# Scan's diagonal part: one masked exponential per direction, and the diagonal itself joined to the skip weight

## The chip, the cores and the metric

One core of a Trainium2 chip runs the whole layer. The metric is the device time of one execution in microseconds (us); lower is better. Before the change it is 2922.42 us, the median of three runs (2921.04 to 2922.88).

## What is computed

The kernel is one layer of a diffusion backbone over 2048 latent tokens (width 1024) and 256 context tokens. A projection feeds two branches: a gated MLP (gMLP) and a Mamba-2 scan (SSD) with 16 heads in two groups, run forwards and backwards over 16 chunks of 128 tokens. Both branches go through one output projection, and a SwiGLU feed-forward follows. What matters here is the scan inside a chunk:

```python
def _ssd_chunked(x, dt, A, bm, cm, h0):
    a = dt * A
    a_cs = jnp.cumsum(a, axis=2)
    xdt = x * dt[..., None]
    seg = a_cs[:, :, :, None] - a_cs[:, :, None, :]
    tri = jnp.tril(jnp.ones((SSD_CHUNK, SSD_CHUNK), dtype=bool))
    decay = jnp.exp(jnp.where(tri, seg, -jnp.inf))
    cb = jnp.einsum('bctgn,bcsgn->bctsg', cm, bm)
    y_diag = jnp.einsum('bctsg,bctsge,bcsgep->bctgep', cb, decay, xdt)
    ...
    y = y_diag + y_off

def _token_mixer(...):
    y, fin_f, fin_b = _ssd_bidirectional(xs, bm, cm, dt_raw, a_log, dt_bias, st_f, st_b)
    y = y.astype(h.dtype) + xs * d_skip[:, None]
```

So for each head the part of `y` inside a chunk is a 128 by 128 matrix times the chunk's `x`. Its entry for a pair of tokens s, t is `cb[t,s]` times the forward term `exp(a_cs[t]-a_cs[s])*dt_f[s]` where s is not after t, plus the mirrored backward term where s is not before t. On the diagonal (s = t) both exponentials are 1.

## The kernel before, in words

The order in which each engine gets its instructions is set when the program is built, by a scheduler that works through the code below; the code's generators (`run`, line 958) say how the main chain of projections and the scan's side chain alternate.

**Projections.** Every large matmul is done three times with split operands (`mm3`, line 224): high by high, high by low, low by high, 24 matmuls of 512 columns for one 128 by 512 output. Their results go to three PSUM banks (`mmp`); everything small uses five others (`smp`). TensorE runs these nearly without a break, and the rest of the kernel lies beside them.

**Conv and scan inputs** (`xbc`, line 474, run for tokens 1024 to 2047 first, then for 0 to 1023). For each 128-channel unit there are the projection, a five-tap convolution on VectorE (line 456), a SiLU, and `finish` (line 481). For the units of C, `finish` also multiplies B by C (lines 498 and 499, four matmuls into one `smp` bank), multiplies the result by a lower and an upper triangular mask on VectorE (line 502, masks with the diagonal) and writes both to a DRAM record `rec` (line 504). `dt_block` (line 401) makes the step sizes `dt_sb`, their running sums `acs`, the negative of the backward sums `nacs`, and the factors `eac`, `ddt`, `tot`; the sums also go to DRAM as rows (`fscr`).

**The scan's output** (`ssd_y`, line 852): 32 items, one for each chunk and group, worked on beside the projections `proj_v`, `proj_u` and `out_half` from about 790 to 1480 us. An item is loaded (`load_rec`, line 727: x, B, C and the two masked products, 1024 columns), then prepared by `y_seg` (line 767), and one item later finished by `y_out` (line 797). `y_seg` works in two quarters of four heads (two quarters an item, 64 in all). For each quarter `f_load` (line 757) fetches two tiles from `fscr`, the forward sums `fb` and the backward sums `bb`, broadcast over the partitions, 256 KB each. For each head of the quarter there are then four short instructions of 128 columns, two on ScalarE (lines 782 and 784) and two on VectorE (lines 783 and 785), and for the quarter one exponential of 512 columns on ScalarE (line 786) and one product on GpSimd (line 787):

```python
S.activation(bb[:, es], bb[:, es], AF.Identity, bias=nacs[:, c, h:h + 1])
V.scalar_tensor_tensor(out=fb[:, es], in0=fb[:, es], scalar=acs[:, c, h:h + 1], in1=bb[:, es], op0=ALU.subtract, op1=ALU.min)
S.activation(A[:, es], rc[:, R_WF:R_WF + P], AF.Copy, scale=dt_sb[:, c, h:h + 1])
V.scalar_tensor_tensor(out=A[:, es], in0=rc[:, R_WB:R_WB + P], scalar=dt_sb[:, c, 16 + h:17 + h], in1=A[:, es], op0=ALU.mult, op1=ALU.add)
```

`y_out` multiplies C by the states (lines 801 and 802), the quarter matrices by x (line 804), scales and adds the parts on VectorE (lines 807, 808, 815, 816, 818), carries the forward state on (lines 812 to 814; line 813 is on GpSimd), and adds the skip `xs*D` (line 817, GpSimd). `y_store` (line 828) transposes and stores. The tiles `tma` come from one ring of 14 that loads, scan and projections share.

## Time and profile before

| | |
|---|---|
| median of 3 runs | 2922.42 us (2921.04 to 2922.88) |
| the profiled execution | 2923.61 us, of which its span is 2921.8 us |
| TensorE (PE) busy | 2803.1 us, 96% of the span |
| VectorE (DVE) busy | 1975.6 us, 68% |
| ScalarE (ACT) busy | 1274.2 us, 44% |
| GpSimd (POOL) busy | 645.4 us, 22% |
| mean granted TensorE clock | 0.98 of full speed |

The page counts an engine as busy while an instruction of it runs; where two overlap in its pipeline the time counts once. "Idle before" is the time that an engine stood still just before an instruction, with what released it. PEclk is the TensorE clock that was granted in a stretch, as a share of 2.4 GHz; it stands at either 2.4 or 1.2 GHz, and 0.96 is a mean over time at the two. SP is the queue that issues most DMAs.

### The profile page before, as it was taken

Reading aid. Unit: us, or ns where it says so; the run is one execution under the profiler, and the core shown is the slowest. Engines: PE = TensorE matmul, PEld = TensorE weight load, DVE = VectorE, ACT = ScalarE, POOL = GpSimd, SP = SyncE. Lnnn points to the kernel's source line nnn. Section 1 sums busy time; section 2 is a strip of 40 time slices with the busy share of each in tenths; the row PEclk is TensorE's granted clock in tenths of the full one; section 3 lists DMA queues with packets and bytes.
Section 4 is the critical chain, followed back from the end, with each engine's and each line's share of the span. In section 5 each row is a group of like instructions: output and inputs, shape, how many; then the busy total and the mean of one; then the engine's idle time right before and its main releaser. Section 6 shows DMA issues by size and latency. Waiting matters only on the chain. (4 is left out here: it accounts for less than half of the span.)

```text
span 2921.8 us, 36695 instructions
## 1 busy us (share of the span) xinstructions
PE 2803.1 (96%) x12478; PEld 2242.7 (77%) x12478; DVE 1975.6 (68%) x3007; ACT 1274.2 (44%) x2361; POOL 645.4 (22%) x555
## 2 busy tenths in 40 slices
PE   7999999999999998998979899999999999999997
PEld 2788778888677776776768688888887788888886
DVE  6776866886678888678676765555876544445556
ACT  4445343344356555444443533333554333333443
POOL 3200000200032233232202444444211222221000
PEclk8999999999999999999989999999999999999998
DMA  6232567743664678787658444445775423334654
GB/s 228 89 94 78 193 226 243 252 127 91 224 187 145 185 253 269 230 268 235 211 178 282 170 156 149 165 154 181 256 249 195 133 102 101 108 109 136 224 192 162
DMA packets 296743, 528.02 MB, mean 181 GB/s; under 512 B 28998, under 2 KB 89830, under 8 KB 296556
## 3 DMA queue, kind: packets, MB, share of 16 engines
q1 hardware_dynamic: 255756, 505.48, 53.0%
q10 hardware_dynamic: 40800, 20.21, 2.4%
q8 instruction: 98, 1.61, 0.2%
q14 instruction: 89, 0.73, 0.1%
HBM read 382.94 MB, written 142.64 MB: 180 GB/s over the span
## 5 line engine op out<-in xcount | busy, mean ns | idle before, releaser
L1065 DVE TENSOR_TENSOR hl<-w,hl 128x1024 fp32r<-128x1024 f32 x286 | 372.1, 1306 | 300.8 <-ACT hl L1064 129.5
L1064 ACT CAST hl<-w 128x1024 fp32r<-128x1024 f32 x286 | 298.8, 1048 | 423.1 <-PE smp L1311 150.0
L234 PE MATMUL mmp<-actt,whi 128*128 128x512 f32 x1120 | 455.7, 407 | 13.3 <-DVE tma L932 8.7
L236 PE MATMUL mmp<-actt,wlo 128*128 128x512 f32 x1120 | 442.1, 395 | 0.0
L235 PE MATMUL mmp<-actt,whi 128*128 128x512 f32 x1120 | 441.5, 394 | 0.2 <-DVE actt L898 0.2
L1179 PE MATMUL mmp<-hl,hl 128*128 128x512 f32 x704 | 276.5, 393 | 2.6 <-ACT t L1204 2.6
L1181 PE MATMUL mmp<-hl,hl 128*128 128x512 f32 x704 | 275.7, 392 | 1.0 <-DVE hl L1065 1.0
L1180 PE MATMUL mmp<-hl,hl 128*128 128x512 f32 x704 | 275.6, 392 | 0.0
L234 PEld LDWEIGHTS mmp<-actt,whi 128*128 128x128 f32 x1120 | 213.7, 191 | 62.0 <-DVE tma L932 9.7
L235 PEld LDWEIGHTS mmp<-actt,whi 128*128 128x128 f32 x1120 | 213.8, 191 | 47.0 <-issue 4.3
L236 PEld LDWEIGHTS mmp<-actt,wlo 128*128 128x128 f32 x1120 | 213.2, 190 | 46.0 <-issue 0.2
L234 PE MATMUL mmp<-whi,actt 128*128 128x512 f32 x512 | 208.9, 408 | 2.9 <-DVE tma L698 2.9
L1180 PE MATMUL smp<-hl,hl 128*128 128x512 f32 x528 | 208.5, 395 | 3.0 <-DVE hl L1065 3.0
L1181 PE MATMUL smp<-hl,hl 128*128 128x512 f32 x528 | 208.2, 394 | 2.5 <-DVE hl L1065 2.5
L1179 PE MATMUL smp<-hl,hl 128*128 128x512 f32 x528 | 209.8, 397 | 0.4 <-ACT hl L1064 0.4
L235 PE MATMUL mmp<-wlo,actt 128*128 128x512 f32 x512 | 206.4, 403 | 0.5 <-DVE wlo L221 0.5
L236 PE MATMUL mmp<-whi,actt 128*128 128x512 f32 x512 | 206.0, 402 | 0.0
L1071 DVE TENSOR_TENSOR t<-smp,t 128x512 f32<-128x512 f32 x88 | 60.5, 687 | 181.1 <-PE smp L1181 131.4
L787 POOL TENSOR_TENSOR tma<-tma 128x512 f32<-128x512 f32 x64 | 93.4, 1461 | 339.4 <-ACT tma L786 138.4
L456 DVE SCALAR_TENSOR_TENSOR tma<-xin,cw,tma 128x512 f32<-128x512 f32 x192 | 144.3, 751 | 25.5 <-ACT tma L454 19.3
L1179 PEld LDWEIGHTS mmp<-hl,hl 128*128 128x128 f32 x704 | 132.7, 189 | 32.5 <-ACT t L1204 3.0
L1071 POOL TENSOR_TENSOR w<-w 128x512 f32<-128x512 f32 x44 | 58.9, 1339 | 446.2 <-DVE hl L1065 290.8
(276 smaller groups left out, 5809.0 us busy)
## 6 DMA issues: line engine op xcount, KB each, us to landing
w<-in_wall_dram SPq DMA_DIRECT2D x110, 512.0 KB, 3.8
ws<-in_wall_dram SPq DMA_DIRECT2D x104, 512.0 KB, 5.0
ascr<-t SPq DMA_DIRECT2D x154, 256.0 KB, 3.9
w<-ascr SPq DMA_DIRECT2D x154, 256.0 KB, 3.3
tma<-fscr SPq DMA_DIRECT2D x128, 256.0 KB, 5.7
w<-wscr SPq DMA_DIRECT2D x88, 256.0 KB, 3.0
t<-x2scr SPq DMA_DIRECT2D x76, 256.0 KB, 4.1
w<-in_wall_dram SPq DMA_DIRECT2D x66, 256.0 KB, 3.1
```

Of the source, the lines that this page charges most:

```text
L234: PE.matmul(ps, lhsT=lh, rhs=rh, start=(i == 0), stop=False)
L235: PE.matmul(ps, lhsT=lh, rhs=rl, start=False, stop=False)
L236: PE.matmul(ps, lhsT=ll, rhs=rh, start=False, stop=(i == n - 1))
L456: V.scalar_tensor_tensor(out=acc[:, :n], in0=raw[:, j:j + n], scalar=cw[:, ch, j:j + 1], in1=acc[:, :n], op0=ALU.mult, op1=ALU.add)
L787: G.tensor_tensor(out=A, in0=A, in1=fb, op=ALU.mult)
L1064: S.copy(hi, x)
L1065: eng.tensor_tensor(out=lo, in0=x, in1=hi.bitcast(F32), op=ALU.subtract)
L1071: eng.tensor_tensor(out=o, in0=a, in1=b, op=ALU.add)
L1179: PE.matmul(ps, lhsT=hi[:, ms_], rhs=t[:, 0, :], start=first and k == 0, stop=False, skip_group_check=not first)
L1180: PE.matmul(ps, lhsT=hi[:, ms_], rhs=t[:, 1, :], start=False, stop=False, skip_group_check=not first)
L1181: PE.matmul(ps, lhsT=lo[:, ms_], rhs=t[:, 0, :], start=False, stop=k == 3, skip_group_check=not first)
```

## The change

It rewrites the quarter of `y_seg` and what feeds it.

- In `finish` the product of B and C is copied once, without masks (ScalarE), and written once to the record, which shrinks from 1024 to 896 columns. The diagonal of the product is made apart: GpSimd multiplies B by C element by element into `dg`, and four matmuls of one column each sum `dg` over its partitions, into the bank that held the product; ScalarE copies the four columns to `cbd`.
- In `dt_block`, `nacs` becomes `ln(dt) - acs` for both directions (one more logarithm), and `dskip = cbd*(dt_f+dt_b) + D` is made for all chunks of the block (three VectorE instructions).
- In `y_seg` each direction gets a tile of 0 and -1e30 added (`cut`, without the diagonal), the forward one on GpSimd, the backward one on VectorE; eight exponentials of 128 columns on ScalarE follow, with `nacs` as bias, then one sum and one product with the record's `cb`, both 512 columns on VectorE. The tile `A` is no longer taken.
- In `y_out` the skip uses `dskip` in place of `D`.

```diff
@@ -75,9 +77,8 @@
-R_WF = 768
-R_WB = 896
-R_N = 1024
+R_CB = 768
+R_N = 896
@@ dt_block
         V.tensor_copy(acs[:, cs, :], v3(pi))
-        V.tensor_scalar(out=nacs[:, cs, :], in0=acs[:, cs, 16:32], scalar1=-1.0, scalar2=None, op0=ALU.mult)
+        V.tensor_scalar(out=v3(e), in0=dt, scalar1=TINY, scalar2=None, op0=ALU.max)
+        S.activation(e[:, :w], e[:, :w], AF.Ln)
+        V.tensor_tensor(out=nacs[:, cs, :], in0=v3(e), in1=acs[:, cs, :], op=ALU.subtract)
+        c8 = slice(c0, c0 + 8)
+        V.tensor_tensor(out=dskip[:, c8, :], in0=dt_sb[:, c8, 0:16], in1=dt_sb[:, c8, 16:32], op=ALU.add)
+        d4 = dskip[:, c8, :].rearrange("p a (g h) -> p a g h", g=2)
+        V.tensor_tensor(out=d4, in0=d4, in1=bc(cbd[:, c8, :].rearrange("p a (g o) -> p a g o", o=1), 8), op=ALU.mult)
+        V.tensor_tensor(out=dskip[:, c8, :], in0=dskip[:, c8, :], in1=row[:, 64:80].rearrange("p (o h) -> p o h", o=1).broadcast_to([P, 8, 16]), op=ALU.add)
@@ xbc, finish
-                    for roff, m in ((R_WF, C_LE), (R_WB, C_GE)):
-                        t = tma()
-                        V.tensor_tensor(out=t[:, :TB].rearrange("p (c x) -> p c x", x=P), in0=ps.rearrange("p (c x) -> p c x", x=P),
-                                        in1=masks[:, m:m + P].rearrange("p (o x) -> p o x", o=1).broadcast_to([P, 4, P]), op=ALU.mult)
-                        DMA.dma_start(rec[q][g][:, :, roff:roff + P].rearrange("c p x -> p c x"),
-                                      t[:, :TB].rearrange("p (c x) -> p c x", x=P))
+                    t = tma()
+                    S.copy(t[:, :TB], ps)
+                    dg = tma()
+                    G.tensor_tensor(out=dg[:, :TB], in0=bt[j][:, :TB], in1=o[:, :TB], op=ALU.mult)
+                    for c in range(4):
+                        PE.matmul(ps[:, c:c + 1], lhsT=dg[:, c * P:(c + 1) * P], rhs=ones[:, 0:1], start=True, stop=True)
+                    S.copy(cbd[:, q * 4:q * 4 + 4, g], ps[:, 0:4])
+                    DMA.dma_start(rec[q][g][:, :, R_CB:R_CB + P].rearrange("c p x -> p c x"),
+                                  t[:, :TB].rearrange("p (c x) -> p c x", x=P))
@@ y_seg
-            A = tma()[:, :TB]
-            for e in range(4):
-                es = slice(e * P, (e + 1) * P)
-                h = h0 + e
-                S.activation(bb[:, es], bb[:, es], AF.Identity, bias=nacs[:, c, h:h + 1])
-                V.scalar_tensor_tensor(out=fb[:, es], in0=fb[:, es], scalar=acs[:, c, h:h + 1], in1=bb[:, es], op0=ALU.subtract, op1=ALU.min)
-                S.activation(A[:, es], rc[:, R_WF:R_WF + P], AF.Copy, scale=dt_sb[:, c, h:h + 1])
-                V.scalar_tensor_tensor(out=A[:, es], in0=rc[:, R_WB:R_WB + P], scalar=dt_sb[:, c, 16 + h:17 + h], in1=A[:, es], op0=ALU.mult, op1=ALU.add)
-            S.activation(fb, fb, AF.Exp)
-            G.tensor_tensor(out=A, in0=A, in1=fb, op=ALU.mult)
-            Gt.append(A)
+            for x, o, eng in ((fb, 0, G), (bb, 16, V)):
+                x3 = x.rearrange("p (e t) -> p e t", t=P)
+                eng.tensor_tensor(out=x3, in0=x3, in1=cuts[0][:, o // 16:o // 16 + 1, :].broadcast_to([P, 4, P]), op=ALU.add)
+                for e in range(4):
+                    es = slice(e * P, (e + 1) * P)
+                    S.activation(x[:, es], x[:, es], AF.Exp, bias=nacs[:, c, o + h0 + e:o + h0 + e + 1])
+            V.tensor_tensor(out=fb, in0=fb, in1=bb, op=ALU.add)
+            f3 = fb.rearrange("p (e t) -> p e t", t=P)
+            V.tensor_tensor(out=f3, in0=f3, in1=rc[:, R_CB:R_CB + P].rearrange("p (o t) -> p o t", o=1).broadcast_to([P, 4, P]), op=ALU.mult)
+            Gt.append(fb)
@@ y_out
-        G.tensor_tensor(out=h3(yb), in0=h3(rc[:, R_X:R_X + TB]), in1=hv(row[:, 64 + g * 8:64 + g * 8 + 8]), op=ALU.mult)
+        G.tensor_tensor(out=h3(yb), in0=h3(rc[:, R_X:R_X + TB]), in1=hv(dskip[:, c, g * 8:g * 8 + 8]), op=ALU.mult)
@@ before the scan's stage
+    cut = hp.tile([P, 2, P], F32, name="cut")
+    for i, m in enumerate((C_LT, C_GT)):
+        V.tensor_scalar(out=cut[:, i, :], in0=masks[:, m:m + P], scalar1=BIG, scalar2=-BIG, op0=ALU.mult, op1=ALU.add)
```

Two places show how the change moves instructions. In the lists L is the line in the kernel at hand (the change's lines are numbered anew), and names are output and input tiles.

TensorE in the first `xbc`, where the one-column matmuls of the first two products stand. Before, the place held projections (L234 to L236) and four transposes (L468):

```order
L235 MATMUL mmp<-actt,whi 128x512
L236 MATMUL mmp<-actt,wlo 128x512
L234 MATMUL mmp<-actt,whi 128x512
L235 MATMUL mmp<-actt,whi 128x512
L468 MATMUL smp<-ident,tma 128x128 x4
L236 MATMUL mmp<-actt,wlo 128x512
L234 MATMUL mmp<-actt,whi 128x512
```

With the change (projections are L235 to L237, the transposes L478, the one-column matmuls L515):

```order
L236 MATMUL mmp<-actt,whi 128x512
L237 MATMUL mmp<-actt,wlo 128x512
L235 MATMUL mmp<-actt,whi 128x512
L515 MATMUL smp<-ones,tma 128x1 x4
L478 MATMUL smp<-ident,tma 128x128 x2
L515 MATMUL smp<-ones,tma 128x1 x4
L478 MATMUL smp<-ident,tma 128x128 x2
L236 MATMUL mmp<-actt,whi 128x512
```

Eight one-column matmuls came in between; nothing went out. They stand 82 and 68 projection matmuls behind the B by C products whose bank they write.

VectorE late in the scan's stage, from the last steps of one item's `y_out` (L823) over an item's `y_seg` to the first step of the next `y_out` (L807). Before:

```order
L823 TENSOR_TENSOR tma<-tma 128x512
L785 SCALAR_TENSOR_TENSOR tma<-rec_sb,dt_sb,tma 128x128
L932 SCALAR_TENSOR_TENSOR tma<-mmp,m_sb,tma 128x512
L783 SCALAR_TENSOR_TENSOR tma<-tma,acs 128x128 x2
L785 SCALAR_TENSOR_TENSOR tma<-rec_sb,dt_sb,tma 128x128
...
L783 SCALAR_TENSOR_TENSOR tma<-tma,acs 128x128
L785 SCALAR_TENSOR_TENSOR tma<-rec_sb,dt_sb,tma 128x128
L932 SCALAR_TENSOR_TENSOR tma<-mmp,m_sb,tma 128x512
L807 TENSOR_TENSOR tma<-smp,eac 128x512
```

With the change (L837 and L821 are the old L823 and L807, L946 the old L932, L265 a sum of squares; L795 adds `cut` to the backward tile, L799 is the sum, L801 the product):

```order
L837 TENSOR_TENSOR tma<-tma 128x512
L795 TENSOR_TENSOR tma<-tma,cut 128x512
L946 SCALAR_TENSOR_TENSOR tma<-mmp,m_sb,tma 128x512
L795 TENSOR_TENSOR tma<-tma,cut 128x512
L799 TENSOR_TENSOR tma<-tma 128x512
L265 TENSOR_TENSOR tma<-tma 128x512
L801 TENSOR_TENSOR tma<-tma,rec_sb 128x512
L799 TENSOR_TENSOR tma<-tma 128x512
L946 SCALAR_TENSOR_TENSOR tma<-mmp,m_sb,tma 128x512
L801 TENSOR_TENSOR tma<-tma,rec_sb 128x512
L821 TENSOR_TENSOR tma<-smp,eac 128x512
```

Sixteen short instructions became six long ones; the first step of the next `y_out` still stands behind the last of them.

## Rows read from the trace of the kernel before

**Rows 1.** The page's first part: busy time, share of the span, instructions.
```profile
PE 2803.1 (96%) x12478; PEld 2242.7 (77%) x12478; DVE 1975.6 (68%) x3007; ACT 1274.2 (44%) x2361; POOL 645.4 (22%) x555
```
**Rows 2.** Busy us (PE, PEld, DVE, ACT, POOL) in first xbc and scan's stage; clock, DMA.
```profile
100.00:280.00 180.00, 179.93 (x962) 154.11 (x961) 130.39 (x191) 82.33 (x153) 8.92 (x57) 0.99 0.30 93
790.00:1480.00 690.00, 649.68 (x2957) 511.16 (x2956) 545.90 (x1094) 362.79 (x973) 202.19 (x155) 0.96 0.71 220
```
**Rows 3.** TensorE's waits, 700 to 1480 us: total us, times, longest.
```profile
PE smp L845 <- DVE tma L807: 5.2, 2, 4.3
PE smp L802 <- DVE tma L807: 5.2, 1, 5.2
PE smp L801 <- issue: 4.6, 1, 4.6
PE mmp L234 <- DVE tma L592: 4.6, 3, 3.2
...
PE smp L804 <- POOL tma L787: 1.1, 1, 1.1
```
**Rows 4.** TensorE in time, first xbc: start, us, line, shape, count.
```profile
120.46 0.40 PE L236 MATMUL mmp<-actt,wlo 128*128 128x512 f32 x1
120.69 1.05 PE L499 MATMUL smp<-tma 128*128 128x128 f32 x8
121.50 0.48 PE L234 MATMUL mmp<-actt,whi 128*128 128x512 f32 x1
121.81 0.40 PE L235 MATMUL mmp<-actt,whi 128*128 128x512 f32 x1
```
**Rows 5.** The same, in an item's `y_out` at 1363 us.
```profile
1363.13 1.89 PE L804 MATMUL smp<-rec_sb,tma 128*128 128x64 f32 x16
1364.86 1.08 PE L812 MATMUL smp<-tma,rec_sb 128*128 128x512 f32 x2
```
**Rows 6.** ScalarE in time, `dt_block` of the second xbc, with the idle time before.
```profile
735.95 1.28 ACT L448 ACT_TABLE_LOAD   x1
740.11 0.38 ACT L448 ACTIVATE ddt<-smp 128x256 f32<-128x256 f32 x1 [2.88 <-PE smp L435]
```
**Rows 7.** VectorE by line, 790 to 1480 us: count, busy us, mean ns, idle before.
```profile
L785 DVE SCALAR_TENSOR_TENSOR tma<-rec_sb,dt_sb,tma 128x128 f32<-128x128 f32 x256 | 101.0, 419 | 15.1 <-ACT tma L784 14.9
L783 DVE SCALAR_TENSOR_TENSOR tma<-tma,acs 128x128 f32<-128x128 f32 x256 | 101.0, 418 | 60.7 <-ACT tma L782 56.8 <-DMA tma<-fscr 3.8
...
L818 DVE TENSOR_TENSOR tma<-tma 128x512 f32<-128x512 f32 x16 | 11.0, 689 | 3.8 <-POOL tma L817 3.4
```
**Rows 8.** ScalarE by line, the same stretch.
```profile
L782 ACT ACTIVATE tma<-tma,nacs 128x128 f32<-128x128 f32 x256 | 88.9, 390 | 91.7 <-DMA tma<-fscr 85.8 <-DMA tma<-hscr 4.7 <-issue 0.9
...
L786 ACT ACTIVATE tma<-tma 128x512 f32<-128x512 f32 x64 | 40.1, 627 | 47.1 <-DVE tma L783 43.1 <-issue 2.8 <-POOL h L813 1.2
```
**Rows 9.** GpSimd by line, the same stretch.
```profile
L787 POOL TENSOR_TENSOR tma<-tma 128x512 f32<-128x512 f32 x64 | 93.4, 1461 | 339.4 <-ACT tma L786 138.4 <-DMA zscr<-tma 75.0 <-DVE tma L785 63.1
```
**Rows 10.** VectorE in time: a run of five long instructions (L903).
```profile
1113.01 3.10 DVE L903 SCALAR_TENSOR_TENSOR actt<-xin,actt 128x512 fp32r<-128x512 f32 x5
```
**Rows 11.** VectorE in time: a run of three short instructions (L785).
```profile
907.96 0.86 DVE L785 SCALAR_TENSOR_TENSOR tma<-rec_sb,dt_sb,tma 128x128 f32<-128x128 f32 x3
```
**Rows 12.** ScalarE in time: a run of four short instructions (L784).
```profile
1370.69 1.28 ACT L784 ACTIVATE tma<-rec_sb,dt_sb 128x128 f32<-128x128 f32 x4 [2.64 <-DVE xin L895]
```
**Rows 13.** ScalarE's waits, 790 to 1480 us: total us, times, longest.
```profile
ACT tma L782 <- DMA tma<-fscr: 85.8, 39, 5.9
```
**Rows 14.** VectorE in time at 1155 us, instructions of 8 and of 128 columns.
```profile
1155.74 1.01 DVE L245 TENSOR_TENSOR sml<-sml 128x8 f32<-128x8 f32 x1
1156.67 0.34 DVE L785 SCALAR_TENSOR_TENSOR tma<-rec_sb,dt_sb,tma 128x128 f32<-128x128 f32 x1
1156.93 0.16 DVE L246 SCALAR_TENSOR_TENSOR sml<-sml 128x8 f32<-128x8 f32 x1
```
**Rows 15.** GpSimd in time, the same stretch.
```profile
1155.56 1.17 POOL L793 TENSOR_TENSOR tma<-rec_sb,ddt 128x512 f32<-128x512 f32 x1 [6.11 <-DVE sml L247]
```

8 lines of the change are left out of this document (7 added, 1 removed).

## The prediction, made before the changed kernel was run

> **What bounds the kernel now.** I read the page first. TensorE is busy for 2803.1 of 2921.8 us, no other engine for more than 1975.6 [rows 1], so time can change only where TensorE gets other instructions or stands still. The view by stretch then shows the two places that the change touches [rows 2]. In the first xbc TensorE is busy for 179.93 of 180 us: VectorE's or ScalarE's work there is hidden, and whatever is added to TensorE counts in full. In the scan's stage, 790 to 1480 us, it is busy for 649.68 of 690 us, so 40.3 us are idle, and its clock stands at 0.96. At two levels of 2.4 and 1.2 GHz that means 2 x 0.04 x 690 = 55 us at half speed, which cost 27.6 us. Together some 68 us lie open. The list of waits says who ends them: ten rows stand for the scan's items, from 5.2 down to 1.1 us, 32.3 us in all, and nearly all name VectorE [rows 3]. They are few and long. VectorE is busy for 545.9 of the 690 us there [rows 2] and works strictly in order, so a late instruction of `y_seg` holds up `y_out` behind it.
>
> **Part 1: the one-column matmuls (TensorE, xbc).** 32 matmuls come in, four for each of eight products. Price: four B by C matmuls of 128 columns are eight rows and took 121.50 - 120.69 = 0.81 us, 0.101 us a row [rows 4]; eight matmuls of 64 columns are sixteen rows and took 1.73 us, 0.108 a row [rows 5]. Halving the columns did not make a row cheaper, so I take the same for one column: 64 rows x 0.108 = 6.9 us. The projection behind such a group starts its successor after 0.31 us where the usual step is 0.23 [rows 4]: 8 x 0.08 = 0.7 us. Sum 7.6 us. If a one-column matmul were one row, it would be 32 x 0.108 + 0.7 = 4.1 us, the lower end. A wait is added too: the group needs ScalarE's copy out of the same bank and GpSimd's product. The order puts 26 to 82 projection matmuls of 0.23 us between, 6 to 19 us, against a copy of at most 0.63 us (the 512 columns of L786) [rows 8] and a product of 1.46 us [rows 9]. I take 0.5 us in all; were ScalarE held up each time by two such copies, 8 x 1.3 = 10 us is the upper end. Behind a waiting group stand the projections themselves, so this would count in full.
>
> **Part 2: edits hidden in xbc and `dt_block`.** Sixteen mask products on VectorE go (689 ns each by the nearest row [rows 7], 11 us) and eight record writes on the SP queue; eight copies on ScalarE and eight products on GpSimd come in. TensorE's 99.96% there [rows 2] hides all of it, so nothing is gained. The logarithm in `dt_block` adds one table load of 1.28 us and a short instruction of some 0.4 us to ScalarE in the first block, and the Exp table is loaded again behind it; in the second only the short one, since the Ln table is there. ScalarE stood idle for 2.88 us there, waiting for TensorE's sums [rows 6], which covers both. Without that cover it would be 1.3 + 1.3 + 0.4 = 3 us once. I take 0.
>
> **Part 3: the quarters of `y_seg` (64).** VectorE: eight short instructions at a step of (0.86 - 0.34)/2 = 0.26 us [rows 11, 14] are 2.1 us; the three long ones, at (3.10 - 0.69)/4 = 0.60 us [rows 10], are 1.8. That is 0.3 us less a quarter, 19 us over the stage. By busy time it is 202 us [rows 7] against 192 x 0.689 = 132, so 70 less; the step is what the engine's queue feels. ScalarE: the exponential of 627 ns goes [rows 8], 40 us; eight short ones stay eight, at a step of 0.30 us [rows 12]. None of the ten waits is ended by ScalarE, so this is worth nothing by itself.
>
> Now the order in time, which decides. Before, ScalarE began as soon as a quarter's tiles had landed; VectorE followed it instruction for instruction and was free 8 x 0.30 + 0.34 = 2.7 us after the landing; the exponential (0.63) and GpSimd's product (1.46) came after VectorE had gone on. The quarter was ready at 4.5 us. With the change GpSimd's addition comes first (1.46), then eight exponentials (2.4), and then two VectorE instructions (2 x 0.6): ready at 5.1 us, and VectorE is free only then, 2.4 us later than before. The scheduler fills the gap with other work (the order shows a sum and an eviction between the additions and the last product), but the first step of the next `y_out` still stands behind. Late landings are the rule: ScalarE waited for `fscr` 39 times, 85.8 us [rows 13]. So the waits that hang on a landing grow. Of the ten I count four such (L802, L845's long one, and both at L804, 1.1 and 3.0 us) and take 1.5 us each, between the 0.6 of the quarter and the 2.4 of VectorE: +6 us. The other six come from VectorE's backlog and shrink by two quarters' 0.3 us each: -3.5 us. Net +2.5 us. Bounds: if every wait of the list grew by 2.4, +24; if the relief emptied the backlog, the 32.3 us and their share of the clock's 27.6 could go in part (below). Smaller records (448 KB in place of 512, 32 times) and fewer `tma` tiles free the SP queue a little; it ended none of the ten waits, so I count nothing.
>
> **Sum.** The profiled execution took 2923.6 us, 1.2 above the median. 2923.6 + 7.6 + 0.5 + 2.5 = 2934.2; against the median that is 2933. I round down by one for the freer ring of tiles: **2932 us**, +0.3%.
>
> **Rivals.**
> - *The relief clears VectorE's queue (faster).* For it: VectorE is the name in nearly all waits, it loses 19 to 70 us of work and 71.7 us of waiting for ScalarE inside the quarters [rows 7], and ScalarE loses 40. If a third of the open 60 us (32.3 + 27.6) goes, -20 + 7.6 gives 2910. It decides from the point where more than 13.4 us go, which makes 7.6 into a gain of over 5.8. Against it: the waits are single events tied to landings, and the saving by step is 0.3 us a quarter.
> - *The two additions exclude each other (slower still).* An 8-column instruction of VectorE that took 0.16 us elsewhere took 1.01 us at 1155.74, and ended at 1156.75, as GpSimd's product ended at 1156.73 [rows 14, 15]. VectorE stood until GpSimd was through. In the change both additions of a quarter become ready together, one on each engine, so VectorE's could wait up to 1.46 us [rows 9] in all 64 quarters, 93 us; the short instructions, 0.34 us undisturbed [rows 14] and 0.419 in the mean [rows 7], paid up to 512 x 0.079 = 40 us for such holds. If each of the ten waits grows by two such holds less the old ones (40 us over 32 items), 2.9 - 1.2 = 1.7 us, that is +17: 2922.4 + 8 + 17 = 2948. The Trainium skill, SBUF — State Buffer, section Who interferes with whom, says that a VectorE instruction with two SBUF inputs contends with a GpSimd instruction that reads SBUF. By that rule all three new VectorE instructions would be open to it; the trace agrees in the 1.01 us above.
> - *Nothing to see.* A one-column matmul is one row (4.1 us), waits as before: 2922 + 4 - 3 = 2923. The same comes out if the change does not do what it says on TensorE, the groups falling into stretches where it stood still anyway; the 179.93 of 180 us speak against that.
>
> **Chances.** A difference below 0.2% (5.8 us) is about what cannot be told from none here. Forecast (2924 to 2942 by itself) 0.43, of which a quarter falls within 0.2%; relief 0.33; exclusion 0.11; nothing to see 0.13. So faster 0.33, same 0.24, slower 0.43. Range 2905 to 2948: down to the relief case with some more, up to the exclusion case; about a tenth lies beyond either end.
>
> **What would show it.** Eight groups of one-column matmuls of 0.8 us in the two xbc with no idle time before them; some 180 us of xbc becoming 184. In the scan's stage VectorE's busy time near 480 us, its added waits before the sum (L799) and named after ScalarE, and L821 as the releaser of TensorE's longest waits. Right about the relief would be a TensorE idle time there below 27 us and a clock of 0.98. Right about exclusion would be VectorE's addition (L795) at over 1.2 us in the mean. I am wrong if the stage's idle time falls by more than 13 us, or if the groups cost under 3 us.

## The result, and the profile after

The changed kernel takes 2963.0 us (median of 4 runs, 2961.2 to 2966.2) against 2921.7 us of the kernel before (2919.7 to 2922.9) on the same chip: a ratio of 1.014, 95% interval 1.0125 to 1.0155. It is slower by 41 us. The prediction had the sign, with a chance of 0.43, and not the size: 2932 us, and no more than 2948 at the upper end.

The page's first part of the changed kernel, busy time by engine, answers to [rows 1]:

```profile
PE 2821.9 (95%) x12542; PEld 2255.9 (76%) x12542; DVE 1954.3 (66%) x2681; ACT 1248.2 (42%) x2317; POOL 662.0 (22%) x563
```

TensorE has its 64 instructions more and is busy for 18.8 us longer; the other 22 us of the 41 are time in which it stands still. VectorE has 326 instructions fewer and is busy for only 21 us less.

Where the time went is read from single instructions that both kernels have: the first B by C products of each xbc, the last sums of each `dt_block` behind it, the last transpose of the scan. These are the rows of those lines in the kernel before (count, shortest/middle/longest ns, first and last start):

```profile
L436 PE MATMUL smp<-tma,ones x2: 432/432/433, 283.6 to 283.9; 128*128 128x320 f32 x2
L499 PE MATMUL smp<-tma x32: 270/275/275, 612.1 to 638.2; 128*128 128x128 f32 x32
L436 PE MATMUL smp<-tma,ones x2: 379/380/382, 739.9 to 740.1; 128*128 128x256 f32 x2
L845 PE MATMUL smp<-ident,sml x4: 269/272/377, 996.3 to 1492.7; 128*8 128x128 f32 x4
```

and of the changed kernel:

```profile
L509 PE MATMUL smp<-tma x32: 272/275/276, 125.4 to 161.7; 128*128 128x128 f32 x32
L439 PE MATMUL smp<-tma,ones x2: 432/432/432, 299.0 to 299.2; 128*128 128x320 f32 x2
L509 PE MATMUL smp<-tma x32: 272/275/275, 630.6 to 659.2; 128*128 128x128 f32 x32
L439 PE MATMUL smp<-tma,ones x2: 379/380/382, 765.5 to 765.7; 128*128 128x256 f32 x2
L859 PE MATMUL smp<-ident,sml x4: 269/272/273, 1023.6 to 1533.7; 128*8 128x128 f32 x4
```

The first group started at 120.7 us before [rows 4] and starts at 125.4 now: 4.7 us are lost ahead of the first changed instruction. From there to the sums of the first `dt_block` it was 162.9 us and is 173.6, +10.7. In the second xbc it was 127.8 and is 134.9, +7.1. Between the two, where nothing changed, +3.1. From the second sums to the last transpose of the scan it was 752.8 and is 768.2, +15.4. Together 41.0; behind the scan nothing is added. The 4.7 us are no fixed part of the change: a second profiled run of the same kernel had its first group at 120.8 us, with the same 173.6 us behind it; it lost 8.6 us between the two xbc instead. What of these 8 us the change brings stays open. The same profile has +8.3 in the second xbc and +24.9 in the scan, in an execution of 2976 us, so the parts of one profile scatter: the first xbc by 0.1 us, the scan by some 10.

So two places have to be explained: xbc with 17.8 us where the prediction had 8.1, and the scan with 15.4 where it had 2.5.

The two stretches of [rows 2], shifted by about the delays above (busy us of PE, PEld, DVE, ACT, POOL; granted clock; DMA share):

```profile
104.70:295.40 190.70, 188.48 (x987) 161.66 (x986) 126.22 (x182) 83.99 (x160) 14.56 (x61) 0.96 0.27 82
816.80:1520.50 703.70, 648.64 (x2958) 508.62 (x2957) 527.40 (x775) 327.24 (x909) 208.62 (x154) 0.96 0.69 213
```

The first xbc has 2.2 us in which TensorE stands still, where it had 0.07, and its clock is 0.96 and no longer 0.99. In the scan's stage TensorE's idle time has grown from 40.3 to 55.1 us at the same clock.

**xbc: the clock falls behind the groups.** TensorE in time, first xbc of the changed kernel (start, us, line, shape, count, idle time before):

```profile
144.09 1.02 PE L515 MATMUL smp<-ones,tma 128*128 128x1 f32 x8
144.97 0.42 PE L478 MATMUL smp<-ident,tma 128*128 128x128 f32 x2
145.69 1.22 PE L515 MATMUL smp<-ones,tma 128*128 128x1 f32 x8 [0.30 <-POOL tma L513]
146.77 0.67 PE L478 MATMUL smp<-ident,tma 128*128 128x128 f32 x2
147.09 0.78 PE L236 MATMUL mmp<-actt,whi 128*128 128x512 f32 x1
147.66 0.63 PE L237 MATMUL mmp<-actt,wlo 128*128 128x512 f32 x1
148.09 0.63 PE L235 MATMUL mmp<-actt,whi 128*128 128x512 f32 x1
...
150.29 0.39 PE L235 MATMUL mmp<-actt,whi 128*128 128x512 f32 x1
```

The group itself costs what was predicted: eight rows from 144.09 to 144.97, 0.88 us. But the projections behind it start 0.43 us after one another, and only from 150.06 on every 0.23 us again. The same in the view by stretch, with the granted clock as the third number from the end:

```profile
147.10:150.10 3.00, 3.00 (x10) 2.37 (x9) 2.00 (x3) 0.01 (x1) 0.00 (x0) 0.54 0.00 0
150.10:153.10 3.00, 3.00 (x21) 2.73 (x20) 0.40 (x1) 1.48 (x2) 0.00 (x0) 1.00 0.01 3
176.50:184.00 7.50, 7.44 (x32) 6.88 (x33) 2.72 (x6) 2.84 (x7) 0.30 (x2) 0.54 0.24 70
667.20:672.10 4.90, 4.90 (x21) 4.03 (x21) 2.37 (x3) 2.49 (x5) 0.19 (x1) 0.65 0.36 104
```

In three places behind the groups TensorE is busy all but throughout and stands at the lower of its two levels, 1.2 GHz, for most of the time. What is lost is the share of the clock that is not granted: 3.0 x 0.46 + 7.5 x 0.46 + 4.9 x 0.35 = 6.5 us. The list of waits has 3.5 us at these matmuls, 3.2 for ScalarE's copy (three times, up to 1.9 us) and 0.3 for GpSimd's product. With eight groups of 0.88 us, 7.0, that is 17.0 of the 17.8 us.

Why the copy is late, and why two groups come together, stands in ScalarE's rows ahead of the longest of these waits, which ended at 176.56 us:

```profile
175.04 0.63 ACT L469 ACTIVATE tma<-tma 128x512 f32<-128x512 f32 x1 [4.53 <-DVE tma L466]
...
175.83 1.08 ACT L511 COPY tma<-smp 128x512 f32<-128x512 f32 x2
```

The copies of two groups stand in ScalarE's queue behind a tanh of the convolution, which waits 4.53 us for VectorE. When it is through, both copies follow at once, and both groups are ready together.

**The scan.** TensorE's waits, 720 to 1520 us (total us, times, longest), for [rows 3]:

```profile
PE smp L656 <- DMA gw<-in_gmw_dram: 10.9, 3, 6.3
PE smp L845 <- DVE tma L837: 10.3, 2, 8.5
PE smp L816 <- DVE tma L821: 8.7, 1, 8.7
PE mmp L235 <- DVE tma L605: 5.9, 3, 2.3
```

Few and long as before, and nearly all on VectorE. The first is not: it is a load of weights of the gated MLP, for which TensorE waited 6.2 us in the kernel before, and what delays it was not followed. VectorE by line in 816.8 to 1520.5 us (count, busy us, mean ns, idle time before and what ended it), for [rows 7]:

```profile
L795 DVE TENSOR_TENSOR tma<-tma,cut 128x512 f32<-128x512 f32 x64 | 62.5, 978 | 85.4 <-DMA tma<-fscr 81.4 <-DMA tma<-hscr 2.4 <-DMA mscr<-tma 1.1
...
L799 DVE TENSOR_TENSOR tma<-tma 128x512 f32<-128x512 f32 x64 | 50.2, 785 | 31.3 <-ACT tma L798 25.1 <-issue 6.2
L801 DVE TENSOR_TENSOR tma<-tma,rec_sb 128x512 f32<-128x512 f32 x64 | 49.2, 769 | 0.7
...
L821 DVE TENSOR_TENSOR tma<-smp,eac 128x512 f32<-128x512 f32 x32 | 21.7, 679 | 0.2 <-DMA mscr<-tma 0.2
```

Two things stand in these rows. Inside the quarters VectorE waits for 85.4 + 31.3 + 0.7 = 117 us, where it waited for 60.7 + 15.1 = 76 [rows 7]. And of four instructions of the same 512 columns the one that reads a sum bank of TensorE takes 679 ns, those with both inputs in SBUF 769 to 978. One of them in time, VectorE's and GpSimd's additions of one quarter:

```profile
1505.36 1.20 DVE L795 TENSOR_TENSOR tma<-tma,cut 128x512 f32<-128x512 f32 x1 [1.38 <-DMA tma<-fscr]
1506.49 0.68 DVE L799 TENSOR_TENSOR tma<-tma 128x512 f32<-128x512 f32 x1
```

```profile
1504.75 1.26 POOL L795 TENSOR_TENSOR tma<-tma,cut 128x512 f32<-128x512 f32 x1 [1.97 <-DMA tma<-fscr]
```

VectorE's addition takes 1.20 us; it ends 0.55 us after GpSimd's has ended at 1506.01. By the profile's times 42 of VectorE's 64 additions lie beside some instruction of GpSimd and take 1133 ns in the mean; the other 22 take 683. The two additions of one quarter overlap in 29 of the 64. VectorE's starts 2.56 us after GpSimd's in the mean (middle value 1.64), and in 39 quarters the landing of its own tile ends the wait.

From the start of GpSimd's addition both are done after 3.54 us in the mean, the eighth exponential after 5.62 and the last product after 8.43. In the kernel before the product was there 7.17 us after the first L782 of its quarter, and VectorE was through with it after 4.82. These two counts do not begin alike: L782 reads the backward tile, GpSimd's addition the forward one, which lands first (by 1.2 us in the 28 quarters where both additions waited for their tiles). Counted from the start of the instruction that reads the backward tile, where its landing ended the wait (41 quarters before, 39 now), the product is there after 6.9 us before and 5.9 now, and VectorE is through after 4.5 and 5.9. So the product is not later than before, but VectorE is held 1.4 us longer.

### The profile page after: what moved, and what is told of

It reads as the page before. It is cut to its first block, busy times and chain, and to the rows that moved or that the text cites. A ratio compares the mean times of both kernels' runs of the same rounds, so it can differ in the third digit from the quotient of the medians.

```text
span 2962.8 us, 36469 instructions
## 1 busy us (share of the span) xinstructions
PE 2821.9 (95%) x12542; PEld 2255.9 (76%) x12542; DVE 1954.3 (66%) x2681; ACT 1248.2 (42%) x2317; POOL 662.0 (22%) x563
## 5 line engine op out<-in xcount | busy, mean ns | idle before, releaser
L235 PE MATMUL mmp<-actt,whi 128*128 128x512 f32 x1120 | 455.8, 407 | 19.5 <-DVE tma L946 13.6
L237 PE MATMUL mmp<-actt,wlo 128*128 128x512 f32 x1120 | 442.6, 395 | 0.0
L236 PE MATMUL mmp<-actt,whi 128*128 128x512 f32 x1120 | 442.4, 395 | 0.0
L235 PEld LDWEIGHTS mmp<-actt,whi 128*128 128x128 f32 x1120 | 214.0, 191 | 69.0 <-DVE tma L946 12.0
L236 PEld LDWEIGHTS mmp<-actt,whi 128*128 128x128 f32 x1120 | 214.1, 191 | 46.4 <-issue 4.3
L237 PEld LDWEIGHTS mmp<-actt,wlo 128*128 128x128 f32 x1120 | 213.6, 191 | 45.8 <-issue 0.2
L798 ACT ACTIVATE tma<-tma,nacs 128x128 f32<-128x128 f32 x512 | 162.5, 390 | 190.3 <-POOL tma L795 153.6
L235 PE MATMUL mmp<-whi,actt 128*128 128x512 f32 x512 | 210.2, 411 | 3.8 <-DVE tma L711 3.8
L236 PE MATMUL mmp<-wlo,actt 128*128 128x512 f32 x512 | 206.9, 404 | 0.6 <-DVE wlo L222 0.6
L237 PE MATMUL mmp<-whi,actt 128*128 128x512 f32 x512 | 206.6, 404 | 0.0
L795 POOL TENSOR_TENSOR tma<-tma,cut 128x512 f32<-128x512 f32 x64 | 89.9, 1406 | 339.4 <-DMA tma<-fscr 201.0
```

The source lines that it names most:

```text
L235: PE.matmul(ps, lhsT=lh, rhs=rh, start=(i == 0), stop=False)
L236: PE.matmul(ps, lhsT=lh, rhs=rl, start=False, stop=False)
L237: PE.matmul(ps, lhsT=ll, rhs=rh, start=False, stop=(i == n - 1))
L798: S.activation(x[:, es], x[:, es], AF.Exp, bias=nacs[:, c, o + h0 + e:o + h0 + e + 1])
```

## The experiments

Three theories at first. For xbc: the groups cost clock and waits beside their work. For the scan: either the two additions exclude each other on VectorE and GpSimd, or the longer chain from landing to product holds VectorE, which works in order. The kernels are named by their edits; ratios are to the kernel before, timed beside each, whose median lay between 2921.2 and 2924.6 us.

| kernel | us | ratio, 95% interval |
|---|---|---|
| the change | 2963.0 | 1.0140 (1.0125 to 1.0155) |
| `xbc_only` | 2934.9 | 1.0049 (1.0031 to 1.0066) |
| `incl` | 2944.8 | 1.0086 (1.0066 to 1.0107) |
| `wide` | 2952.2 | 1.0101 (1.0078 to 1.0124) |
| `incl_dve` | 2913.2 | 0.9967 (0.9955 to 0.9978) |
| `incl_swap` | 2941.7 | 1.0061 (1.0042 to 1.0079) |
| `incl_pool` | 2955.3 | 1.0102 (1.0078 to 1.0125) |
| `dve_hold` | 2940.2 | 1.0060 (1.0039 to 1.0080) |
| `before_dve` | 2912.9 | 0.9963 (0.9953 to 0.9973) |
| `after_dve` | 2933.4 | 1.0044 (1.0025 to 1.0062) |
| `incl_tail` | 2919.2 | 0.9985 (0.9975 to 0.9995) |
| `dve_xact` | 2908.2 | 0.9946 (0.9931 to 0.9961) |
| `dve_skip` | 2896.1 | 0.9917 (0.9894 to 0.9940) |
| `after_again` | 2967.1 | 1.0159 (1.0140 to 1.0177) |
| `wide_again` | 2958.6 | 1.0117 (1.0100 to 1.0134) |
| `before_skip` | 2910.9 | 0.9967 (0.9955 to 0.9979) |
| `dve_skip_xact` | 2893.6 | 0.9904 (0.9888 to 0.9921) |

### The two halves apart: `xbc_only` and `incl`

`xbc_only` is the kernel before with this put behind its two mask products:

```diff
+                    dg = tma()
+                    G.tensor_tensor(out=dg[:, :TB], in0=bt[j][:, :TB], in1=o[:, :TB], op=ALU.mult)
+                    for c in range(4):
+                        PE.matmul(ps[:, c:c + 1], lhsT=dg[:, c * P:(c + 1) * P], rhs=ones[:, 0:1], start=True, stop=True)
+                    S.copy(cbd[:, q * 4:q * 4 + 4, g], ps[:, 0:4])
```

> The kernel before with the eight groups of one-column matmuls (GpSimd's product, 4 matmuls, ScalarE's copy of the sums) and nothing else of the change; the sums are not used. Theory 1 (the groups cost work, waits and clock): the profile of the change shows, after the one-column groups in the two xbc, stretches in which a projection matmul steps at 0.43 us in place of 0.23, about 17 us of half clock that the kernel before has not, which is 8.5 us, beside 7.6 us of work and 3.5 us of waits at these matmuls. So 15 to 20 us slower than before, 2937 to 2942, with half-clock stretches in xbc behind the groups and the scan's stage within 4 us of before. Theory 2 (only the work counts, and the clock of those stretches is chance): 8 us slower, 2930. Theory 3 (the groups fall beside other work): 2922.

It is slower by 13.7 us. By the same instructions as above its first xbc takes 6.1 us more and its second 5.4, 11.5 in all, and the scan's stage nothing. So the groups do cost time by themselves, but not quite as expected: the clock does not fall behind any of the eight groups. TensorE in time shows what is different (first xbc of `xbc_only`):

```profile
142.55 1.02 PE L510 MATMUL smp<-ones,tma 128*128 128x1 f32 x8
143.44 0.47 PE L236 MATMUL mmp<-actt,wlo 128*128 128x512 f32 x1
...
144.68 0.40 PE L235 MATMUL mmp<-actt,whi 128*128 128x512 f32 x1
144.91 0.95 PE L510 MATMUL smp<-ones,tma 128*128 128x1 f32 x8
145.72 0.48 PE L236 MATMUL mmp<-actt,wlo 128*128 128x512 f32 x1
146.04 0.39 PE L234 MATMUL mmp<-actt,whi 128*128 128x512 f32 x1
```

Here six projections of 512 columns stand between two groups. In the change, in the three places, the groups come in pairs, with a few transposes, one or two projections or a stand of up to 1.9 us between or ahead of them. This kernel's groups need no copy out of their bank, only VectorE's mask products. So of the 11.5 us, 7 are work and 1.5 waits at the groups. 0.4 us is a wait for the convolution, and 1.7 us is lost to a stretch at the lower clock from 269.5 to 272.9 us, which stands behind matmuls of 32 columns ahead of the sums of `dt_block` and not behind a group. Some 0.9 us is not accounted for.

`incl` is the changed kernel without the groups. Both masks keep their diagonal, where each exponential gives its own step; the two add up to what the diagonal needs, and the skip weight is the old one:

```diff
-    for i, m in enumerate((C_LT, C_GT)):
+    for i, m in enumerate((C_LE, C_GE)):
...
-        G.tensor_tensor(out=h3(yb), in0=h3(rc[:, R_X:R_X + TB]), in1=hv(dskip[:, c, g * 8:g * 8 + 8]), op=ALU.mult)
+        G.tensor_tensor(out=h3(yb), in0=h3(rc[:, R_X:R_X + TB]), in1=hv(row[:, 64 + g * 8:64 + g * 8 + 8]), op=ALU.mult)
```

with `dg`, the sums, `cbd` and `dskip` gone.

> The changed kernel without the groups: the masks of both directions keep their diagonal, where both exponentials give the step alone, so the skip weight stays as before and no sums are needed; y_seg is the changed one. Theory 1 (xbc cost some 19 us, the order of y_seg some 14, the rest lies in the start): 2941 to 2947, xbc as before, the scan's stage 10 to 18 us longer than before. Theory 2 (only the groups' work of 8 us goes): 2955. Theory 3 (the loss was all in xbc, the scan's part is drift): 2918 to 2926.

2944.8, as the first theory had it. Both xbc last as before within 0.3 us, and the scan's stage is 18 us longer in the profiled run. The two halves, 13.7 and 23.7 us, make 37 of the 41 us.

### Is it the clock: `wide`, and once more `wide_again` and `after_again`

```diff
-                        PE.matmul(ps[:, c:c + 1], lhsT=dg[:, c * P:(c + 1) * P], rhs=ones[:, 0:1], start=True, stop=True)
-                    S.copy(cbd[:, q * 4:q * 4 + 4, g], ps[:, 0:4])
+                        PE.matmul(ps[:, c * P:(c + 1) * P], lhsT=dg[:, c * P:(c + 1) * P], rhs=ones, start=True, stop=True)
+                    S.copy(cbd[:, q * 4:q * 4 + 4, g], ps.rearrange("p (c x) -> p c x", x=P)[:, :, 0])
```

> The changed kernel with 128 columns of ones in place of one in the sums of the diagonal: as many rows of matmuls, 128 times the columns. Theory 1 (a row has one price, and it is the narrow rows that the lower clock follows): the groups still cost 0.8 us each, but the half-clock stretches behind them go, so 5 to 9 us faster than the change, 2954 to 2958. Theory 2 (the clock falls for the waits at the group or for the break in the projections): as the change, 2963. Theory 3 (columns have a price of their own here): slower than the change, 2966 or more.

2952.2, 10.8 us below the change. The pair of groups at the place of the rows shown above now reads

```profile
139.06 1.13 PE L515 MATMUL smp<-ones,tma 128*128 128x128 f32 x8
140.66 1.16 PE L515 MATMUL smp<-ones,tma 128*128 128x128 f32 x8 [0.47 <-POOL tma L513]
141.65 0.60 PE L478 MATMUL smp<-ident,tma 128*128 128x128 f32 x4
142.01 0.48 PE L236 MATMUL mmp<-actt,whi 128*128 128x512 f32 x1
```

with the same pairing and a wait between, 0.99 us for a group in place of 0.88, and the projections some 0.23 us apart behind it. At the other three places the order is another: the two groups stand back to back, sixteen rows. So this kernel differs from the change in where its groups stand as well as in their columns. Its profiled run lay 11 us below its own median, so both kernels were timed once more, side by side:

> The change as it is, in one call with the kernel that has the 128-column sums. 2961 to 2966 us. With it the difference to the other is free of the call.

> The change with 128 columns of ones in the sums. If the half-clock stretches behind the one-column groups cost 8.5 us, it lies 6 to 12 us below the change of the same call, and its profile has no stretch at half clock between a group and the end of its xbc. If they cost nothing of their own, within 3 us of the change.

2967.1 and 2958.6: 8.5 us apart. Behind the groups of the first xbc neither profile of `wide` has a stretch at the lower clock; the second xbc had none in the one and one in the other, so it is not stopped entirely. The second profile of the change has four, two in each xbc, where the first had three. (Both profiles of `wide` have another one, at 266.6 and 266.9 us, behind the matmuls of 32 columns ahead of the sums of `dt_block`; it belongs to no group.)

Sums of 128 times as many columns gained 8 to 11 us, though each group costs 0.1 us more. By the same instructions as above, 5.0 us of it lie in the first xbc and 0.5 in the second, and 5.0 and 0.1 in the second pair of profiles. The rest lies between the two xbc and in the scan, and no run shows that it comes from the groups. That the one column is what the lower clock follows is likely, but not shown, since columns and places changed together.

### The scan: who adds

`incl_dve`, `incl_swap` and `incl_pool` change one line of `incl`:

```diff
-            for x, o, eng in ((fb, 0, G), (bb, 16, V)):
+            for x, o, eng in ((fb, 0, V), (bb, 16, V)):      # incl_dve
+            for x, o, eng in ((fb, 0, V), (bb, 16, G)):      # incl_swap
+            for x, o, eng in ((fb, 0, G), (bb, 16, G)):      # incl_pool
```

> As the kernel with both diagonals kept in the masks, and the forward addition on VectorE too, so that GpSimd has none. Theory A (the scan's loss is the two additions excluding each other): VectorE's addition falls from 0.98 us in the mean to under 0.72, and the time falls by 8 us or more against that kernel. Theory B (the loss is the order in time: VectorE, in order, waits for the landing and again for the exponentials): the wait in front of the sum stays, the quarter is ready some 0.1 us earlier, the time within 4 us of that kernel. Theory C (VectorE's amount of work binds): 64 x 0.69 = 44 us more of it less 64 x 0.29 = 19 us of holds makes it slower by 5 us or more.

> As the kernel with both diagonals in the masks (2944.8 us), with the two additions changing engines: VectorE adds the forward cut, whose exponentials come first, GpSimd the backward one. Both are still ready together, one on each engine. Theory A (exclusion): nothing changes, 2938 to 2950, VectorE's addition still at 0.9 us or more in the mean. Theory B (the length of the chain from landing to product): ScalarE starts some 0.6 us earlier and GpSimd's addition is covered by the forward exponentials, as with both on VectorE, so 2913 to 2925. Theory C (GpSimd, in order, stands at the landing and its later products come late): as with A in time, 2938 to 2950, but VectorE's mean may fall.

> As the kernel with both diagonals in the masks (2944.8 us), with both additions on GpSimd. Theory A (exclusion with VectorE's addition): VectorE has no addition to be held, so the time falls below 2940 unless its other two-input instructions pay the same holds. Theory B (length of the chain): the second addition ends some 1.4 us later, the quarter is ready 0.2 to 1.4 us later, so 2945 to 2965. Theory C (GpSimd's queue): 64 x 1.4 = 90 us more of work in that queue, slower, 2955 or more.

`incl_dve` is 31.6 us faster than `incl`, and faster than the kernel before. It gives VectorE 64 instructions more. VectorE by line in `incl_dve` (800 to 1530 us):

```profile
L783 DVE TENSOR_TENSOR tma<-tma,cut 128x512 f32<-128x512 f32 x124 | 91.2, 742 | 71.1 <-DMA tma<-fscr 70.2 <-DMA gmscr<-tma 0.4
...
L789 DVE TENSOR_TENSOR tma<-tma,rec_sb 128x512 f32<-128x512 f32 x64 | 45.9, 716 | 0.5
L787 DVE TENSOR_TENSOR tma<-tma 128x512 f32<-128x512 f32 x63 | 45.7, 725 | 18.8 <-ACT tma L786 18.4
...
L809 DVE TENSOR_TENSOR tma<-smp,eac 128x512 f32<-128x512 f32 x32 | 21.9, 684 | 0.7 <-PE smp L803 0.7
```

against `incl`, same view and stretch:

```profile
L783 DVE TENSOR_TENSOR tma<-tma,cut 128x512 f32<-128x512 f32 x62 | 59.5, 963 | 86.1 <-DMA tma<-fscr 83.6 <-DMA tma<-hscr 2.4
...
L789 DVE TENSOR_TENSOR tma<-tma,rec_sb 128x512 f32<-128x512 f32 x62 | 48.2, 777 | 0.6
L787 DVE TENSOR_TENSOR tma<-tma 128x512 f32<-128x512 f32 x62 | 47.7, 770 | 27.0 <-ACT tma L786 20.4 <-issue 6.3 <-POOL tma L783 0.2
...
L809 DVE TENSOR_TENSOR tma<-smp,eac 128x512 f32<-128x512 f32 x32 | 21.8, 681 | 0.2 <-DMA mscr<-tma 0.2
```

All three kinds with two inputs in SBUF get shorter, 963 to 742, 777 to 716, 770 to 725 ns, and the one that reads a sum bank stays. Sorted by whether an instruction of GpSimd runs at the same time, all `TENSOR_TENSOR` of 128x512 on VectorE (790 to 1480 us of `incl`) show it more plainly: with both inputs in SBUF 1085 ns beside GpSimd (97 of them) and 686 otherwise (217), with a sum bank as one input 681 and 680. The Trainium skill, SBUF — State Buffer, section Who interferes with whom, says that a VectorE instruction with two SBUF inputs contends with a GpSimd instruction that reads SBUF, and that one with at most one SBUF input, outside the two-port modes, does not. The trace agrees, with 963 against 742 ns for the one kind and 681 against 684 for the other.

A number for the whole stage: for each VectorE instruction from 790 us to the scan's last `y_out`, the time above the fastest tenth of its own shape, added up. It is 69.1 us in `incl` and 33.6 in `incl_dve`. And the chain of a quarter gets shorter: both additions are done 2.08 us after the first starts (3.63 in `incl`), the eighth exponential is through after 4.15 (5.67), the last product after 6.72 (8.57). A part of this is the count itself, which begins with GpSimd's start in `incl` and with VectorE's, when it is free, in `incl_dve`.

`incl_swap` is where both theories had a say. ScalarE does start its exponentials earlier, after 0.78 us and not 1.33 (middle value), and still nothing is gained, 2941.7. GpSimd's addition takes 1.54 us in the mean there, both are done only after 3.32, the eighth exponential after 5.50. So it was not that GpSimd's addition stood first in ScalarE's way; it is that one of the two is GpSimd's at all. `incl_pool`, without any addition on VectorE, is slower yet, 2955.3: its other instructions are held instead (the sum and the product 832 ns each), and VectorE waits in front of the sum for 131.8 us. It is no verdict between A and C, whose expectations both leave room for it.

### The reading without the chain, the chain's end in place of its head: `dve_hold` and `incl_tail`

`dve_hold` adds to `incl_dve`, in every quarter, reads of GpSimd that nobody waits for:

```diff
+            r3 = rc[:, R_X:R_X + TB].rearrange("p (a t) -> p a t", t=P)
+            for _ in range(2):
+                G.tensor_tensor(out=cuts[1], in0=r3[:, 0:2, :], in1=r3[:, 2:4, :], op=ALU.add)
```

> As the kernel with both additions on VectorE (2913.2 us), with two additions of 128x256 a quarter given to GpSimd that read the record, wait for no landing of the quarter and whose result nobody uses: GpSimd's reads without its place in the chain. Theory A (exclusion): a good part of the 31.6 us comes back, 2925 or more, and VectorE's instructions with two inputs in SBUF are longer again by some 0.05 to 0.2 us in the mean. Theory B (chain) and theory C (waiting in GpSimd's queue): within 4 us of 2913.

It costs 27 us: 2940.2. GpSimd's row and VectorE's addition in `dve_hold` (800 to 1500 us):

```profile
L783 POOL TENSOR_TENSOR spare<-rec_sb 128x256 f32<-128x256 f32 x121 | 121.4, 1003 | 179.5 <-DMA rec_sb<-rec 172.5
```

```profile
L786 DVE TENSOR_TENSOR tma<-tma,cut 128x512 f32<-128x512 f32 x123 | 99.2, 818 | 65.6 <-DMA tma<-fscr 65.4
```

The lengthening of VectorE's instructions goes from 33.6 to 64.0 us, and the time follows: +30 and +27. The chain of a quarter hardly moves (4.29 us to the eighth exponential, 4.15 in `incl_dve`). GpSimd's own queue is no explanation: VectorE waits for it in the state's sum for 2.3 us in all, and at the skip product for 5.5 (5.8 in `incl_dve`).

`incl_tail` is `incl_dve` with `G` for `V` in the last product of a quarter.

> As the kernel with both additions on VectorE (2913.2 us), with the last product of a quarter on GpSimd, where the kernel before had its product: as much of GpSimd's work as in the changed y_seg, but behind the exponentials and not ahead of them. Theory A1 (the amount of GpSimd's reading beside VectorE counts, wherever it stands): 2935 to 2947. Theory A2 (it counts by what VectorE does at that moment, and at the landing it has the two-input addition of the same quarter): 2915 to 2930, near the kernel before; VectorE's addition stays under 0.78 us in the mean.

2919.2, the time of theory A2. GpSimd has as much work in the stage as in `incl` (208 us, 205 there) and VectorE as many instructions, but the lengthening is 53.8 us in place of 69.1 and the eighth exponential is through after 4.40 us in place of 5.67. The mean of VectorE's addition, 807 ns, is above what A2 allowed. So the same amount of GpSimd's work costs some 26 us more at the landing than behind the exponentials (29 by the two ratios). The lengthening alone does not put the kernels in order: counted the same way it is 53.5 us in `incl_swap`, which takes 2941.7, and 53.9 here; it is 62 in the kernel before and 63 in the change. So the holds did not grow in sum from before to after; where GpSimd's instruction stands in the quarter matters too, and how much of the loss is holds and how much is place is not separated.

### The kernel before, the change, and further that way

`before_dve` is the kernel before with one letter changed, the product of L787 on `V`. `after_dve` is the change with the forward addition on `V`.

> The kernel before with its one GpSimd product of a quarter (the exponential times the weighted record) on VectorE in place of GpSimd, nothing else of the change. Theory A (GpSimd beside VectorE is what costs): 93 us of GpSimd's work go, VectorE gets 64 x 0.69 = 44 us and loses some 20 to 40 us of holds, and the product is ready 0.8 us sooner, so 2900 to 2916. Theory D (the gain of both additions on VectorE came from the new form's shorter list of instructions): 2922 or slower, since VectorE now has 500 instructions and 44 us more.

> The changed kernel as it is, groups of one-column matmuls and all, with one letter changed: the forward addition on VectorE. If the two costs are separate (the groups 14 to 19 us in xbc, GpSimd beside VectorE 31.6 us in the scan), it lies at 2927 to 2935 against 2963 of the change, and at 6 to 14 us above the kernel before. If the groups' cost was only seen because the scan's stage was late too, 2913 to 2920. If the scan's loss needs the groups, 2945 or more.

2912.9 and 2933.4. The old form gains from less GpSimd too, by 11.7 us, so GpSimd's place beside VectorE was a cost before the change; and the change, whole but for GpSimd in the quarter, is 9.2 us slower than before, 20 us above `incl_dve` (22 by the two ratios). The two costs are separate and add up within the scatter: the groups cost 18 us beside `incl`, 20 beside `incl_dve`, 14 in the kernel before.

`dve_xact` takes `incl_dve` and gives the weighted inputs (`xd`) to ScalarE, `dve_skip` the skip product to VectorE, `dve_skip_xact` does both, and `before_skip` is `before_dve` with the skip product on VectorE:

```diff
-            G.tensor_tensor(out=h3(xd), in0=h3(rc[:, R_X:R_X + TB]), in1=hv(ddt[:, c, g * 8:g * 8 + 8]), op=ALU.mult)
+            for e in range(8):
+                es = slice(e * HD, (e + 1) * HD)
+                S.activation(xd[:, es], rc[:, R_X + e * HD:R_X + (e + 1) * HD], AF.Copy, scale=ddt[:, c, g * 8 + e:g * 8 + e + 1])
...
-        G.tensor_tensor(out=h3(yb), in0=h3(rc[:, R_X:R_X + TB]), in1=hv(row[:, 64 + g * 8:64 + g * 8 + 8]), op=ALU.mult)
+        V.tensor_tensor(out=h3(yb), in0=h3(rc[:, R_X:R_X + TB]), in1=hv(row[:, 64 + g * 8:64 + g * 8 + 8]), op=ALU.mult)
```

> As the kernel with both additions on VectorE (2913.2 us), with one more product taken from GpSimd: the inputs weighted by the step (30 times, 1.27 us) as eight ScalarE scalings of 64 columns each, some 2.2 us. Theory A (GpSimd's reading beside VectorE is what costs): a third of GpSimd's remaining 111 us in the stage goes, and by the 27 us that 121 us of spare reading cost, some 8 us are won: 2903 to 2909. Theory E (ScalarE's order takes the gain back: eight short instructions stand between the exponentials): 2912 to 2920.

> As the kernel with both additions on VectorE (2913.2 us), with the skip product (32 times, 1.15 us) on VectorE too. Theory A by the same price: 37 us less of GpSimd's reading is worth 8 us, and VectorE gets 32 x 0.69 = 22 us more but waits 6 us less for GpSimd there: 2907 to 2914. Theory C (VectorE's amount of work binds by now): 2916 or more.

> The kernel before with the last product of a quarter and the skip product on VectorE: the old y_seg with as little GpSimd as the kernel with additions and skip on VectorE (2896 us). If the new form of y_seg costs nothing by itself, 2892 to 2902. If the old form is better (VectorE is free earlier after a landing), 2890 or less; if the new one is better (it has 38 us less of VectorE's work), 2903 to 2913.

> Additions and skip product on VectorE, the weighted inputs on ScalarE: GpSimd keeps the 30 products of the state alone, some 38 us. If GpSimd's reading still costs VectorE time (26.6 us of lengthening beside it in the kernel of 2896 us, a half of which would go), 2884 to 2892; if ScalarE's or VectorE's order binds by now, 2894 to 2902.

`dve_xact` gains 5 us on `incl_dve`, inside the 2903 to 2909 of theory A. `dve_skip` gains 17 us (15 by the two ratios) where 0 to 6 were expected: 2896.1. VectorE's lengthening there is 31.8 us, hardly below the 33.6 of `incl_dve`, so the price per GpSimd instruction does not explain this gain. In `dve_xact` it falls to 17 us, for a gain of 5. What else does is open; the skip product's two waits, VectorE's for GpSimd and GpSimd's for VectorE, sit in the middle of `y_out`, and both are gone. `dve_skip_xact`, 2893.6, is the fastest of all, 1% below the kernel before, and not clearly faster than `dve_skip`; it falls between the two times that were expected.

`before_skip`, 2910.9, gains nothing over `before_dve` and lies where the new form was expected to be the better one. With GpSimd out of the way to the same degree the new form of `y_seg` is thus 15 us faster than the old one (2896.1), while with one addition on GpSimd it is 17 to 24 us slower than the kernel before.

## Why the prediction was wrong

**Part 1, the groups: right in the work, short by the clock and the waits.** The work came out as said, 0.88 us a group, 7.0 us. The step that failed is "I take 0.5 us in all" for the wait, with "against a copy of at most 0.63 us": measured 3.5 us, and the projections that the order put between did not cover it, since the copies stood in ScalarE's queue behind a tanh that waited for VectorE. And the sum had no term for the clock: 6.5 us in the profiled run. In `wide`, whose clock falls behind one pair of groups at most, the two xbc are 5 to 5.5 us shorter, with 0.9 us more of work in the groups. The clock was in the prediction for the scan alone; for xbc it was taken as 0.99 and left. The upper end of that part, 7.6 + 10, is about the 17.8 measured, but by another mechanism than the two copies it was made from.

**Part 2** held: both xbc of `incl` last as before, so the copies, the products saved and the logarithm are hidden.

**Part 3: VectorE beside GpSimd was left at its undisturbed price.** The net of +2.5 was +15.4 (+24.9 in the second profile); the stated bound was +24. The step that failed is the relief, the "70 less" of VectorE's busy time and "the other six" waits that were to shrink by it. The forecast priced VectorE's new instructions at 689 ns, or a step of 0.60 us, whatever GpSimd did; the holds stood in the rival alone. Measured: 527 us of VectorE in the stage where 480 were expected, and 30 of these 47 us because the three instructions took 769 to 978 ns. With the forward addition on VectorE 31.6 us came back, and GpSimd's reads alone cost 27.

The order had a wrong step as well. "GpSimd's addition comes first (1.46), then eight exponentials (2.4)" has the two additions side by side and 3.9 us to the eighth exponential. Measured 5.62 us in the mean: 2.56 until VectorE's addition starts, mostly behind its own tile, 0.98 for it, 2.08 for the last exponentials. But from the landing of the backward tile VectorE is held 1.4 us longer than before, less than the 2.4 of the prediction, so what was too small is not this price; the relief that was to stand against it did not come. Two smaller things: one of the ten waits that were counted as the scan's (L234 behind L592, 4.6 us) is an eviction of the gated MLP, and the wait for the gated MLP's weights, left aside, grew from 6.2 to 10.9 us. How the 15.4 us divide between holds, place and that load stays open.

**The rivals.** "The two additions exclude each other" had 0.11 and was right that GpSimd holds VectorE: taking GpSimd out of the additions gave back 31.6 us, and reads alone cost 27. Its picture, both additions of a quarter ready together, fits 29 of 64 quarters. That its price for the scan, +17, is near the 15.4 measured is partly luck: it was added up from holds that grow, and in sum they stayed at 62 to 63 us. Its total of 2948 is short by what xbc cost and by the 8 us outside both places. The mark set for it, VectorE's addition at over 1.2 us in the mean, was too high: 0.98. "The relief clears VectorE's queue" had 0.33 and did not come: idle time rose from 40.3 to 55.1 us. It was not wrong about the form: with as little on GpSimd (`dve_skip` against `before_skip`) the new form is 15 us faster than the old one. "Nothing to see" failed in both its parts.

**The range** was too narrow at the top because its upper end took one bad case, and two came together: 10 us more than forecast in xbc, 13 us more in the scan. The 8 us ahead of and between the two xbc, which no part of the prediction had, come on top.

## What to carry to other kernels

Where VectorE sets the pace, count GpSimd's instructions as a cost to it: beside them VectorE's instructions with two SBUF inputs took 1085 ns and not 686, and at the head of the quarter, behind the landing, the same work of GpSimd cost 26 us more than at its end. Here 64 additions on GpSimd in place of VectorE lost 31.6 us, and moving the skip product to VectorE as well won 17 more, for a reason that is open. Count two chains from the same landing before comparing them. And where TensorE has no idle time, price a new narrow matmul by what stands behind it: look at the granted clock after it, at what separates two such groups, and at the pieces that each has to wait for.

## What the runs showed of the hardware that was not expected

- Eight rows of 128 columns take 0.99 us where eight of one column take 0.88, and the kernel with 128 is 8.5 us faster, 5 of them in the two xbc: behind pairs of one-column groups the projections ran at 1.2 GHz in three places, though TensorE was busy for 7.44 of 7.50 us in the longest; in `xbc_only`, with six projections of 512 columns between two groups, behind none.
- Reads of GpSimd that no instruction waits for, 121 us of them in the stage, made the kernel 27 us slower.
- VectorE's instructions that read one input from a sum bank kept 679 to 684 ns in every kernel, whatever GpSimd did.
